# A hybrid encoder layer on one core: the input norm moves behind the projections as a factor per token

## The chip, the cores and the metric

The kernel runs on one core of a Trainium2 chip. The metric is the time of one execution in microseconds (us) on the device. Engines are named as the profile names them: PE (the matrix engine, with its weight loads PEld), DVE (VectorE), ACT (ScalarE), POOL (GpSimd) and SP, whose queue issues most transfers. Each engine works through its own instructions in a fixed order and waits where an operand is not there yet.

## The reference

2304 tokens of width 1024 (2048 of one request, 256 of another) go through one layer and a final norm, all in float32:

```
h = rmsnorm(x, norm1_w);  p = h @ w_in          # mq mk mv mo (512 each), gates 32, aq 512, ak 128, av 128
m_out = mlstm_mixer(mq, mk, mv, mo, gates, ...) # 8 heads, both directions
    # i, f from gates + b_gates;  v from mv;  out = sigmoid(mo) * norm(h_f + h_b) * mh_norm_w
a_out = attention_mixer(aq, ak, av, ...)
    # q = rope(rmsnorm(aq, q_norm_w)), k = rope(rmsnorm(ak, k_norm_w)) per head of 64;  8 query heads, 2 of keys
x = x + concat(m_out, a_out) @ w_out
h = rmsnorm(x, norm2_w);  x = x + (silu(g) * a) @ w_down,  [a, g] = conv3(h @ w_up)
y = rmsnorm(x, final_norm_w)
rmsnorm(x, w) = x * rsqrt(mean(x * x) + 1e-6) * w
```

## The kernel before

Every large matmul is done as three products of rounded parts (high x high, high x low, low x high), so each operand is kept as a pair. The token tiles are 128 wide: 18 of them, `order` = 16, 17 (the short request), then 0 to 15.

The first stage is `phase_a`. For each tile `front(i)` loads x with channels on the partitions (from `xT`, 512 bytes in a row), squares it on ACT (L183), adds the eight channel chunks on POOL (L189, L190; for the first tile on DVE, L186), sums over the partitions with a matmul by ones (L128), takes the power -1/2 on POOL (L142), spreads the result over the partitions with a second matmul (L144), multiplies x by it on DVE (L192), and splits that into the pair `n1T` (L193 on ACT, L194 on DVE). The pair is stored to `n_d` for the mLSTM part (L195) and used at once by `mm` (L236): 48 matmuls per tile, 24 of 512 columns and 24 of 288, into one PSUM tile `pj`, of which there are two. `weights` loads and splits the eight chunks `w_a` (L104, L105, L109); the same lines split the mLSTM weights `wm` later.

`post1` works on `pj`: it copies q and k to SBUF (L244), splits v (L247, L248), adds the gate bias (L251), squares q and k (L254), sums per head (L256), takes the power on POOL (L97, L98), multiplies (L258), and rotates: the cosine products on DVE (L264), four sine products on POOL (L270), their sum on DVE (L272). Then q and k are split (L274, L275, L278, L279) and stored. `post2` transposes k (L309). `gates` works on the gates of four tiles at a time, transposes them (L302) and copies the result into `rows` (L303). `tables` and `tables2` build the rotation tables `tab` (L214 to L223). `gate_math` follows the last tile: two scans over `rows` (L354, L356), transposes (L390), and the tables for the mLSTM.

After that two streams share the engines. `mlstm` handles four pairs of heads; `proj` reads `n_d` back and makes `mj` (L698, keys and queries) and `mv` (L708, values and the output gate `og`, L712), `proj_kv` and `proj_qo` do the same for the last pair. `attention` works in blocks of 512 queries: scores `ps` (L563, L564), row maxima `px` (L540, L542), exponentials (L567 to L569), values `pv` (L580 to L582), result to `mix_d`. When the mLSTM is finished, `phase_c` multiplies by `w_out`: 8 loads `cmx` of `mix_d` (L940, L941) and 192 matmuls `po` (L963) for each of nine blocks of 256 tokens, then adds x (L970), and norms (`rs_c`, L128, L144, L975 to L982). The first matmuls of the up-projection (`pa`, `pb`, `pc`, L1120) come between them and after them.

What stands where on an engine is set by a scheduler, which simulates the program with costs of its own and writes down one list per engine; `run_both` deals out the steps of the two streams by fixed numbers. A change of any instruction's cost in the simulation can therefore move others far behind it.

## Time and profile before

| | us |
|---|---|
| median of three runs (lowest, highest) | 3363.43 (3363.26, 3368.52) |
| the profiled execution, its own time | 3364.37 |
| its span | 3362.7 |
| PE busy | 3256.9 (97%) |
| DVE busy | 2473.1 (74%) |
| ACT busy | 1993.4 (59%) |
| POOL busy | 603.9 (18%) |

The times in the prediction's rows count from the start of the span. A row of the timeline gives start, length, engine, line, operation, tile written and read, number of instructions, and in brackets the idle time ahead of it with what ended it. A row of a line gives the shortest, median and longest duration in ns. A row of a stretch gives its length, then per engine the busy time and the number of instructions, the clock granted to PE, the busy share of the DMA engines and the rate in GB/s.

### The profile page before, as it was taken

The numbers are of one execution on the slowest core, as the hardware profiler recorded it, in microseconds if no ns is written. First come the engines' busy times: TensorE is split into PE (matmuls) and PEld (weight loads), VectorE is DVE, ScalarE is ACT, GpSimd is POOL, SyncE is SP. The second block draws the span as 40 slices with busy tenths as digits, with TensorE's granted clock in tenths as the row PEclk, the third lists the DMA queues.
The fourth block names the chain that finished last, engine by engine and source line by source line (L and its number), as shares of the span: only waits on it lengthen the run. The fifth ranks groups of instructions, "written<-read, shape, count | busy, mean of one in ns | idle before, by whom it ended". The sixth has DMA issues, their size and how long they took to land.

```text
span 3362.7 us, 53401 instructions
## 1 busy us (share of the span) xinstructions
PE 3256.9 (97%) x19566; PEld 3034.9 (90%) x19566; DVE 2473.1 (74%) x3736; ACT 1993.4 (59%) x3708; POOL 603.9 (18%) x1001
## 2 busy tenths in 40 slices
PE   7989999999999999999998899999999999999998
PEld 6778888888888888789887899999999999999998
DVE  7874576677657768876565899998888888666664
ACT  4535666666666776664444556665667667554543
POOL 7774032213215322200000000000000000020101
PEclk9999999999999999999998999999999999999999
DMA  8756343343337343332225656667666657968673
GB/s 247 215 182 186 106 124 93 107 126 102 103 102 237 111 131 121 122 115 95 86 96 184 239 208 223 219 239 275 227 238 236 212 192 258 317 225 277 225 241 114
DMA packets 393878, 601.68 MB, mean 179 GB/s; under 512 B 31248, under 2 KB 254640, under 8 KB 393616
## 3 DMA queue, kind: packets, MB, share of 16 engines
q1 hardware_dynamic: 360304, 552.51, 49.2%
q0 software_dynamic: 11856, 33.96, 3.7%
q10 hardware_dynamic: 21456, 11.80, 1.2%
q8 instruction: 154, 2.52, 0.3%
q14 instruction: 108, 0.88, 0.1%
HBM read 434.23 MB, written 163.92 MB: 178 GB/s over the span
## 4 chain that ended last, share of the span: by engine, by line
PE 77%; issue 6%; DMA 5%; POOL 4%; DVE 4%; ACT 3%; SPq 0%; POOLq 0%; DVEq 0%; ACTq 0%
PE pa L1120 16%; PE pc L1120 8%; PE po L963 6%; PE pf L1379 5%; PE pb L1120 4%; PE mj L698 4%; PE mv L708 4%; PE pv L580 3%; PE ps L563 3%; PE pv L582 3%; PE pv L581 3%; PE ps L564 3%; PE ph L1379 3%; PE px L540 3%; PE pg L1379 2%
## 5 line engine op out<-in xcount | busy, mean ns | idle before, releaser
L569 DVE TENSOR_TENSOR xx<-pe,xx 128x1024 fp32r<-128x1024 f32 x260 | 321.3, 1236 | 154.3 <-ACT xx L568 152.9
L567 ACT ACTIVATE pe<-ps 128x1024 f32<-128x1024 f32 x260 | 266.3, 1024 | 241.4 <-PE ps L564 237.8
L542 DVE TENSOR_REDUCE mx<-px 128x1 f32<-128x1024 f32 x256 | 310.6, 1218 | 88.2 <-PE px L540 86.4
L1337 POOL TENSOR_TENSOR sq<-sq,sq 128x384 f32<-128x384 f32 x38 | 49.5, 1303 | 1375.5 <-ACT sq L1333 1229.4
L568 ACT ACTIVATE xx<-pe 128x1024 fp32r<-128x1024 f32 x260 | 275.1, 1058 | 5.6
L963 PEld LDWEIGHTS po<-cmx,wo 128*128 128x128 f32 x1728 | 235.7, 193 | 38.3 <-ACT cmx L940 12.7
L963 PE MATMUL po<-cmx,wo 128*128 128x256 f32 x1728 | 244.0, 286 | 18.3 <-ACT cmx L940 12.1
L1124 ACT ACTIVATE u<-pa 128x386 f32<-128x386 f32 (+2 forms) x264 | 129.2, 490 | 173.7 <-PE pa L1120 170.2
L563 PE MATMUL ps<-qq,kk 128*128 128x512 f32 x520 | 213.0, 410 | 8.2 <-ACT pe L567 3.2
L580 PE MATMUL pv<-xx,vv 128*128 128x512 f32 x520 | 211.6, 407 | 3.4 <-ACT xx L568 2.0
L582 PE MATMUL pv<-xx,vv 128*128 128x512 f32 x520 | 211.7, 407 | 2.4 <-DVE xx L569 2.3
L581 PE MATMUL pv<-xx,vl 128*64 128x512 f32 x520 | 208.2, 400 | 0.0
L564 PE MATMUL ps<-qm,kl 65*128 65x512 f32 x520 | 206.5, 397 | 0.0
L698 PEld LDWEIGHTS mj<-mn,wm 128*128 128x128 f32 x1296 | 179.9, 193 | 20.1 <-ACT og L712 6.2
L698 PE MATMUL mj<-mn,wm 128*128 128x256 f32 x1296 | 192.1, 288 | 3.8 <-ACT og L712 3.7
L708 PE MATMUL mv<-wm,mn 128*128 128x256 f32 x1296 | 190.8, 285 | 0.7 <-ACT qb L704 0.7
L708 PEld LDWEIGHTS mv<-wm,mn 128*128 128x128 f32 x1296 | 176.5, 190 | 14.5 <-ACT qb L704 1.0
L236 PE MATMUL pj<-w_a,n1T 128*128 128x512 f32 (+1 forms) x864 | 178.8, 361 | 10.0 <-DVE n1T L194 6.7
L236 PEld LDWEIGHTS pj<-w_a,n1T 128*128 128x128 f32 x864 | 144.0, 196 | 30.2 <-DVE n1T L194 7.6
L540 PE MATMUL px<-kk,qq 128*128 128x512 f32 x512 | 166.6, 406 | 3.4 <-ACT pe L567 1.7
L802 ACT ACTIVATE dm<-dm,tm 128x128 f32<-128x128 f32 x288 | 95.8, 392 | 95.9 <-POOL dm L799 90.0
L1120 PE MATMUL pc<-nt,wb 128*128 128x386 f32 (+2 forms) x792 | 147.8, 341 | 0.0
(333 smaller groups left out, 8246.9 us busy)
## 6 DMA issues: line engine op xcount, KB each, us to landing
mn<-n_d SPq DMA_DIRECT2D x216, 256.0 KB, 3.2
ru<-w_up SPq DMA_DIRECT2D x88, 512.0 KB, 5.2
rs<-wsu_d SPq DMA_DIRECT2D x88, 512.0 KB, 5.6
act_d<-ts SPq DMA_DIRECT2D x33, 768.0 KB, 6.1
nt<-act_d SPq DMA_DIRECT2D x60, 384.0 KB, 5.0
re_t<-wsd_d SPq DMA_DIRECT2D x45, 512.0 KB, 5.0
wsu_d<-tw SPq DMA_DIRECT2D x44, 512.0 KB, 4.3
act_d<-ya SPq DMA_DIRECT2D x99, 192.0 KB, 2.8
```

The source lines that it names most:

```text
L236: nc.tensor.matmul(pjs[t][:, c0:c1], nTs[tiles[t]][:, c, a, :], ws[c][:, b, c0:c1], start=(c == 0 and k == 0), stop=(c == NCC - 1 and k == 2))
L542: nc.vector.tensor_reduce(s.mx[:, t0, z0:z0 + 1], ps, AX.X, ALU.max)
L563: nc.tensor.matmul(o, kk[:, kc:kc + P], s.qq, start=True, stop=False)
L569: nc.vector.tensor_tensor(x[:, 1], pe, f32(x[:, 0]), ALU.subtract)
L580: nc.tensor.matmul(s.pv, vv[:, kt % 4, :], x1, start=kt == 0, stop=False)
L581: nc.tensor.matmul(s.pv[0:HD], vl[:, kt % 4, :], x1, start=False, stop=False)
L582: nc.tensor.matmul(s.pv, vv[:, kt % 4, :], x2, start=False, stop=kt == s.nk - 1)
L698: nc.tensor.matmul(pj[:, o], s.w[c][:, a, o * P:(o + 1) * P], nT[c][:, h, :], start=(c + o + k == 0), stop=(c == NCC - 1 and k == 2 and o ...
L708: nc.tensor.matmul(pv[:, o], nT[c][:, a, o * P:(o + 1) * P], s.w[c][:, h, 256:512], start=(c + o + k == 0), stop=(c == NCC - 1 and k == 2 ...
L963: nc.tensor.matmul(po[:, o], wo[c][z // 2][:, a, n], mx[c][:, h, :], start=c + o + k == 0, stop=c == NCC - 1 and o == 1 and k == 2)
L1120: s.nc.tensor.matmul(p, w[:, aa, c, :], ops[k][:, c, bb, 0:s.n], start=c == 0 and i == 0 and not add, stop=c == NCC // 2 - 1 and i == 2, s ...
L1379: nc.tensor.matmul(ps[c], w[:, aa, c, :], t[:, gi - g0, bb, 0:H], start=gi == 0 and m == 0 and not more, stop=gi == NG - 1 and m == 2, ski ...
```

## The change

`front` no longer norms: it loads x from a copy with 4096 bytes in a row per partition (`xA`), and splits it. The 1/rms of a token, `g.rt`, comes from a second load of x with tokens on the partitions (`xR`), squared and summed by one ACT instruction; three small POOL instructions follow. Since `norm1_w` is already in the weights, every projection comes out too large by the token's rms, and the factor is applied afterwards: to v and the gates in `post1`, to the mLSTM's v and output gate in `proj`, `vback` and `proj_qo`, and as a logarithm (`g.lnr`) to the gates' exponents for the keys and to `nm` for the queries. The norm of q and k takes up the factor by a changed epsilon. The rotation reads `pj` in PSUM, its sine products are on DVE, and the norm's factor comes after the sum. `n_d` is stored in rows of 1024 bytes instead of 512. There are three PSUM tiles `pj`. The first two tiles' matmuls are issued together, weight chunk by weight chunk, and `mm` of a tile is issued one tile earlier than before.

```diff
         def front(i):
...
-            nc.sync.dma_start(x, g.xT[b, :, :, c0:c0 + P])
-            xq = sx.tile([P, NCC, P], F32, tag="xq", name=f"xq{i}", bufs=2)
-            nc.scalar.activation(xq, x, AF.Square, scale=1.0 / 32.0)
...
-                for k in (4, 2):
-                    nc.gpsimd.tensor_tensor(xq[:, 0:k], xq[:, 0:k], xq[:, k:2 * k], ALU.add)
-                nc.gpsimd.tensor_tensor(sq, xq[:, 0], xq[:, 1], ALU.add)
-            r = rstd_bc(g, sf, pp if n else pj_, [sq], P, "rs" if n else "pj", f"a{i}", bufs=2)
-            nc.vector.tensor_tensor(x, x, r.unsqueeze(1).to_broadcast([P, NCC, P]), ALU.mult)
+            nc.sync.dma_start(x, g.xA[i])
             nc.scalar.activation(nT[:, :, 0, :], x, AF.Copy)
             nc.vector.tensor_tensor(nT[:, :, 1, :], x, f32(nT[:, :, 0, :]), ALU.subtract)
-            g.st.dma_start(g.n1_d[b, :, :, :, c0:c0 + P], f32(nT))
+
+        def norm(i):
+            b, o = i // 2, i % 2
+            xr = sx.tile([P, D], F32, tag="xr", name=f"xr{i}", bufs=2)
+            nc.sync.dma_start(xr, g.xR[i])
+            g.st.dma_start(g.n1_d[b, :, :, o], f32(nTs[i]))
+            z = sp.tile([P, 2], F32, tag="ms1", name=f"ms1_{i}", bufs=4)
+            nc.scalar.activation(xr, xr, AF.Square, scale=1.0 / 32.0, accum_out=z[:, 0:1])
+            nc.gpsimd.tensor_scalar(z[:, 0:1], z[:, 0:1], EPS, None, ALU.add)
+            nc.gpsimd.tensor_scalar(z[:, 1:2], z[:, 0:1], EPS, None, ALU.mult)
+            nc.gpsimd.tensor_tensor(g.rt[:, i:i + 1], z[:, 0:1], g.mhalf[:, 0:1], ALU.pow)
+            ms1[i] = z
...
         def post1(i, pj):
-            nc.scalar.activation(qk, pj[:, 0:640].rearrange("p (h d) -> p h d", d=HD), AF.Copy)
+            u = pj[:, 0:640].rearrange("p (h d) -> p h d", d=HD)
+            nc.scalar.activation(xh, u, AF.Square, scale=0.125)
...
-            nc.vector.tensor_tensor(xh, qk, r.unsqueeze(2).to_broadcast([P, 10, HD]), ALU.mult)
...
-                nc.vector.tensor_tensor(t1[:, h0:h1, :], xh[:, h0:h1, :],
+                nc.vector.tensor_tensor(t1[:, h0:h1, :], u[:, h0:h1, :],
                                         tab[:, ti, a, 0:1, :].to_broadcast([P, n, HD]), ALU.mult)
...
-                    nc.gpsimd.tensor_tensor(half(t2[:, h0:h1, :], q), half(xh[:, h0:h1, :], 1 - q),
+                    nc.vector.tensor_tensor(half(t2[:, h0:h1, :], q), half(u[:, h0:h1, :], 1 - q),
                                             sin.to_broadcast([P, n, 2, 16]), ALU.mult)
             nc.vector.tensor_tensor(t1, t1, t2, ALU.add)
+            nc.vector.tensor_tensor(t1, t1, r.unsqueeze(2).to_broadcast([P, 10, HD]), ALU.mult)
...
         def gates(i0, n):
+            nc.scalar.activation(g.lnr[:, i0:i0 + n], g.rt[:, i0:i0 + n], AF.Ln)
...
-                nc.vector.tensor_copy(g.rows[:, :, i * P:(i + 1) * P], pg)
+                nc.scalar.activation(g.rows[:, :, i * P:(i + 1) * P], pg, AF.Copy)
...
     def proj(s, b):
...
-        nc.scalar.activation(og, pv[:, :, P:BT], AF.Tanh, scale=0.5)
+        for o in range(2):
+            nc.scalar.activation(og[:, o], pv[:, o, P:BT], AF.Tanh, scale=g.rh[:, 2 * b + o:2 * b + o + 1])
...
     def proj_qo(s, b):
...
-        nc.scalar.activation(og, pj[:, 1], AF.Tanh, scale=0.5)
+        rb = s1.tile([P, 2, P], F32, tag="og", name=f"rb{b}", bufs=1)
+        nc.sync.dma_start(rb, g.nm_d[2 * b:2 * b + 2, 16].unsqueeze(0).to_broadcast([P, 2, P]))
+        nc.vector.tensor_tensor(og, pj[:, 1], rb.rearrange("p n t -> p (n t)"), ALU.mult)
+        nc.scalar.activation(og, og, AF.Tanh, scale=0.5)
```

How the lists of the engines change shows at three places. (A number behind an underscore tells tiles of one name apart, and x3 is three instructions of one kind; the first tile's pair is `n1T_147` before and `n1T_151` after.) First, PE at the start of the program, before:

```order
L128 MATMUL rs_a_153<-ones,sq_151 128x2
L144 MATMUL rs_a_153<-ident,rcol_a_155 128x128
L236 MATMUL pj_248<-w_a_131,n1T_147 128x512 x2
L128 MATMUL rs_a_180<-ones,sq_176 128x2
L236 MATMUL pj_248<-w_a_131,n1T_147 128x512
L236 MATMUL pj_248<-w_a_131,n1T_147 128x288 x3
L236 MATMUL pj_248<-w_a_132,n1T_147 128x512 x3
L236 MATMUL pj_248<-w_a_132,n1T_147 128x288 x3
```

and after, where `pj_237` is the second tile's:

```order
L237 MATMUL pj_236<-w_a_135,n1T_151 128x512 x3
L237 MATMUL pj_236<-w_a_135,n1T_151 128x288 x3
L237 MATMUL pj_236<-w_a_136,n1T_151 128x512 x3
L237 MATMUL pj_236<-w_a_136,n1T_151 128x288 x3
L237 MATMUL pj_237<-w_a_135,n1T_161 128x512 x2
L237 MATMUL pj_236<-w_a_137,n1T_151 128x512
L237 MATMUL pj_237<-w_a_135,n1T_161 128x512
L237 MATMUL pj_237<-w_a_135,n1T_161 128x288 x3
```

The norm's matmuls are gone, and the second tile follows the first chunk by chunk.

Second, DVE ahead of the split of the fourth tile. Before, this is `n1T_297`, behind two norm multiplications (L192) and work of the first two tiles (`t_16`, `xh_436`, `gp`):

```order
L192 TENSOR_TENSOR x_298<-x_298,rs_a_306 128x1024
L295 SCALAR_TENSOR_TENSOR gtm<-gtm,t_16_460 128x2x16
L192 TENSOR_TENSOR x_401<-x_401,rs_a_409 128x1024
L258 TENSOR_TENSOR xh_436<-qk_429,rqk_440 128x640
L109 SCALAR_TENSOR_TENSOR wm_7_2448<-rm_7_0_2477,nw,wm_7_2448 128x512
L298 COPY gp_129<-gtm 128x4x8
L298 COPY gp_130<-gtm 128x4x8
L194 TENSOR_TENSOR n1T_297<-x_298,n1T_297 128x8x128
```

and after, `n1T_334`:

```order
L266 TENSOR_TENSOR t_17_464<-pj_237,tab 128x512
L272 TENSOR_TENSOR t_16_364<-pj_236,tab 128x16x16 x2
L266 TENSOR_TENSOR t_16_363<-pj_236,tab 128x128
L272 TENSOR_TENSOR t_16_364<-pj_236,tab 128x4x16 x2
L109 SCALAR_TENSOR_TENSOR wm_0_2312<-rm_0_0_2320,nw,wm_0_2312 128x512
L109 SCALAR_TENSOR_TENSOR wm_1_2313<-rm_1_0_2324,nw,wm_1_2313 128x512
L290 SCALAR_TENSOR_TENSOR t_16_481<-gtm 128x32
L184 TENSOR_TENSOR n1T_334<-x_335,n1T_334 128x8x128
```

The split no longer has the norm's multiplications ahead of it, but rotation products of both first tiles and two weight splits.

Third, PE where the attention ends (its last three instructions are L580 to L582 before, L593 to L595 after), before:

```order
L580 MATMUL pv_12_19778<-xx_12_7_19972,vv_16_12_10656 128x512
L581 MATMUL pv_12_19778<-xx_12_7_19972,vl_16_12_10657 64x512
L582 MATMUL pv_12_19778<-xx_12_7_19972,vv_16_12_10656 128x512
L144 MATMUL rs_c_20580<-ident,rcol_c_20583 128x128 x2
L963 MATMUL po_0_20481<-cmx_7_20441,wo_0_17320 128x256
L963 MATMUL po_1_20482<-cmx_7_20441,wo_0_17320 128x256
```

and after:

```order
L593 MATMUL pv_12_19712<-xx_12_7_19906,vv_16_12_10550 128x512
L594 MATMUL pv_12_19712<-xx_12_7_19906,vl_16_12_10551 64x512
L595 MATMUL pv_12_19712<-xx_12_7_19906,vv_16_12_10550 128x512
L983 MATMUL po_3_19951<-cmx_3_19223,wo_1_17163 128x256 x2
L983 MATMUL po_3_19951<-cmx_4_19227,wo_1_17189 128x256 x3
L983 MATMUL po_3_19951<-cmx_5_19231,wo_1_17199 128x256 x3
L983 MATMUL po_3_19951<-cmx_6_19235,wo_1_17245 128x256 x3
```

Before, the next matmuls use `cmx_7_20441`, which is loaded from what the last attention block wrote. After, the rest of one block of `po` (38 matmuls), a whole block (192) and 84 matmuls of a third stand between the attention's end and the tile that needs its result; 614 matmuls `po` are left at that point, against 300 before. The last block's norm, `rs_c`, had 44 matmuls `pa` and `pb` between it and the last `po`, and now none: they stand ahead of the last block.

More of the change, by code (lines that the diff above doesn't have):

```diff
@@ L226, in mm @@
         def mm(*tiles):
-            pjs = [pj_.tile([P, 1024], F32, tag="pj", name=f"pj{i}", bufs=2) for i in tiles]
+            pjs = [pj_.tile([P, 1024], F32, tag="pj", name=f"pj{i}", bufs=3) for i in tiles]
             cols = ((0, 512), (512, 800))
@@ L313, in phase_a @@
         front(order[0])
-        weights(range(0, 3))
+        weights(range(0, 2))
         front(order[1])
-        weights(range(3, 6))
+        weights(range(2, NCC))
         front(order[2])
-        weights(range(6, NCC))
+        for i in order[0:2]:
+            norm(i)
         tables()
         tables2(slice(0, 2))
+        norm(order[2])
+        pjs = mm(*order[0:2])
         prev = None
         for n, i in enumerate(order):
-            pj, = mm(i)
+            if 0 < n < NT - 1:
+                pjs += mm(order[n + 1])
             if n + 3 < NT:
                 front(order[n + 3])
+                norm(order[n + 3])
                 if n + 4 == NT:
@@ L692, in proj @@
         nm = f"{s.p}_{b}"
-        nT = [sn.tile([P, 2, BT], F32R, tag="nT", name=f"mn{nm}_{c}", bufs=NTB) for c in range(NCC)]
+        nT = [sn.tile([P, 2, 2, P], F32R, tag="nT", name=f"mn{nm}_{c}", bufs=NTB) for c in range(NCC)]
         for c in range(NCC):
@@ L718, in proj_halves @@
         nm = f"{s.p}_{b}"
-        nT = [sn.tile([P, 2, BT], F32R, tag="nT", name=f"{name}n{nm}_{c}", bufs=NTB) for c in range(NCC)]
+        nT = [sn.tile([P, 2, 2, P], F32R, tag="nT", name=f"{name}n{nm}_{c}", bufs=NTB) for c in range(NCC)]
         for c in range(NCC):
```

68 lines of the change are left out of this document (39 added, 29 removed).

## The prediction

> **What bounds the kernel now.** I read the stretches of 100 us first, then PE's timeline where PE isn't full.
>
> ```profile
> 0.00:100.00 100.00, 76.12 (x380) 64.08 (x381) 81.22 (x129) 50.03 (x72) 76.61 (x96) 0.95 0.78 234
> 100.00:200.00 100.00, 90.61 (x511) 78.03 (x510) 84.63 (x147) 49.52 (x83) 80.02 (x91) 0.98 0.72 212
> 200.00:300.00 100.00, 91.17 (x644) 83.34 (x643) 56.44 (x98) 38.85 (x90) 72.39 (x136) 0.97 0.71 215
> ...
> 1400.00:1500.00 100.00, 92.58 (x524) 75.40 (x523) 78.00 (x130) 63.85 (x104) 7.28 (x13) 0.98 0.28 90
> ...
> 1800.00:1900.00 100.00, 73.22 (x475) 71.69 (x474) 66.48 (x115) 33.88 (x52) 4.38 (x6) 0.85 0.77 270
> ```
>
> The columns are PE, PEld, DVE, ACT and POOL busy, then the clock granted to PE, the DMA share and GB/s. PE is busy for 3256.9 of 3362.7 us; of the 105.8 us of idle time, 42 lie in the first 300 us and 27 in the stretch from 1800. So the change pays where it fills these holes, and elsewhere only what PE itself does counts.
>
> ```profile
> 14.46 1.22 PE L236 MATMUL pj<-w_a,n1T 128*128 128x512 f32 x2 [2.40 <-ACT n1T L193]
> ...
> 24.54 4.01 PE L236 MATMUL pj<-w_a,n1T 128*128 128x512 f32 x20
> 33.16 7.90 PE L236 MATMUL pj<-w_a,n1T 128*128 128x512 f32 x22 [4.61 <-DVE n1T L194]
> ...
> 59.58 7.15 PE L236 MATMUL pj<-w_a,n1T 128*128 128x512 f32 x25 [1.14 <-DVE n1T L194]
> ...
> 157.26 6.67 PE L236 MATMUL pj<-w_a,n1T 128*128 128x512 f32 x30
> 163.77 0.38 PE L144 MATMUL rs_a<-ident,rcol_a 128*128 128x128 f32 x2
> ...
> 164.11 6.73 PE L236 MATMUL pj<-w_a,n1T 128*128 128x288 f32 x36
> ...
> 220.62 3.51 PE L698 MATMUL mj<-mn,wm 128*128 128x256 f32 x28
> ```
>
> The projections run from 14.5 to 220.6 us. In undisturbed stretches they are fast: 66 matmuls (42 of 512 columns, 24 of 288) take 6.65 + 6.57 us, 0.222 and 0.162 us each, so a tile's 24 + 24 need 9.2 us and 18 tiles 166. The fourth tile starts in earnest at 59.6, and the last fifteen take (220.6 - 59.6) / 15 = 10.73 us each. The mLSTM's `mj` follows without a gap, so the end of this stage is what counts for all that follows.
>
> **The start.** `front` now waits for no sum, power or multiplication.
>
> ```profile
> 5.78 1.06 ACT L183 ACTIVATE xq<-first 128x1024 f32<-128x1024 f32 x1 [3.70 <-DMA first<-xT]
> 22.10 1.74 DVE L214 COPY rot<-qkw 128x16 f32<-128x16 f32 x8 [0.78 <-DMA qkw<-q_norm_w]
> L194 DVE TENSOR_TENSOR n1T<-x,n1T x16: 1204/1218/1776, 43.9 to 202.7; 128x1024 fp32r<-128x1024 f32 x16
> L109 DVE SCALAR_TENSOR_TENSOR w_a<-first,nw,w_a 128x800 fp32r<-128x800 f32 x6 | 6.5, 1092 | 0.0
> L109 DVE SCALAR_TENSOR_TENSOR wm<-rm,nw,wm 128x512 fp32r<-128x512 f32 x8 | 7.7, 980 | 1.4 <-ACT wm L105 1.4
> L223 DVE TENSOR_TENSOR tab<-tab,qkw 128x128 f32<-128x128 f32 x6 | 3.0, 500 | 0.0
> 35.00:40.00 5.00, 5.00 (x16) 3.93 (x15) 2.92 (x2) 1.15 (x2) 4.83 (x5) 0.63 0.90 261
> ```
>
> x lands at 5.8; a split on ACT (1.06, the same size), one on DVE (1.2) and a weight split (1.09) give the first matmul near 9.5 instead of 14.5. DVE needs 2 x 1.2 + 8 x 1.09 = 11.1 us for both pairs and all weights, less than the 18.4 us of the 96 matmuls, so these are PE's own: the first two tiles end near 28.5 (before: 24.54 + 4.01 for one), the third at 37.7. Then comes a hole. The rotation tables now queue behind two loads of x (0.52 MB each) and one `n_d` (1.05 MB), which at 299 GB/s (below) is 7 us, so `rot` starts near 28.5 instead of 22.1. DVE then does `rot` and two scalings (2.3), twelve table products (6.0), the first tiles' parts that stand ahead of `n1T_334` (two reductions, five or six products, two `wm` splits; by the rows here and below 8.6 with the split itself): it is ready at about 45. PE idles for 7 us, and then pays for a lowered clock: in the stretch 35 to 40, after an idle 4.6 us, 0.63 was granted, and 22 matmuls took 7.90 us instead of 4.9, a price of 3.0. The page TensorE: Matmul & The Clock Gate of the Trainium skill (What's actually happening) has half clock after about 3.4 us of idling until about 3.4 us of work are done. The trace agrees in kind; by the page the price would be an estimated 1.7 us, and the two such holes of this sum would cost 2.6 us less. At 59.58 the kernel before paid 7.15 - 25 x 0.222 = 1.6 of the same kind. Lead at the fourth tile: 59.6 - 45 - (3.0 - 1.6) = 13 us.
>
> **The steady tiles.** On PE, 36 + 36 norm matmuls go: the two of L144 hold up the next by 0.14 us (163.77 to 163.91), and L128 the same. What stays beside the 9.2 us is `pk` and `pg`, like them 0.14 each: 9.5 us; with the 0.95 to 0.98 granted above, 9.75. Can DVE keep up? Shortest, median and longest ns, then means by shape:
>
> ```profile
> L264 DVE TENSOR_TENSOR t<-xh,tab x34: 275/819/1666, 45.0 to 221.7; 128x512 f32<-128x512 f32 x17, 128x128 f32<-128x128 f32 x17
> L272 DVE TENSOR_TENSOR t<-t,t x17: 804/826/1908, 48.7 to 223.7; 128x640 f32<-128x640 f32 x17
> L256 DVE TENSOR_REDUCE ms<-xh x18: 801/806/821, 33.3 to 226.3; 128x10 f32<-128x640 f32 x18
> L275 DVE TENSOR_TENSOR qz<-t,qz x17: 672/680/777, 50.3 to 225.3; 128x512 fp32r<-128x512 f32 x17
> L279 DVE TENSOR_TENSOR kz<-t,kz x17: 274/284/1373, 50.9 to 226.0; 128x128 fp32r<-128x128 f32 x17
> L248 DVE TENSOR_TENSOR v<-pj,v x18: 229/278/294, 33.0 to 224.8; 128x128 fp32r<-128x128 f32 x18
> L264 DVE TENSOR_TENSOR t<-xh,tab 128x128 f32<-128x128 f32 x17 | 11.7, 687 | 0.0
> L270 POOL TENSOR_TENSOR t<-xh,tab 128x256 f32<-128x256 f32 x34 | 34.4, 1033 | 10.3 <-DVE xh L258 10.3
> L98 POOL TENSOR_TENSOR rqk<-rqk,mhalf 128x10 f32<-128x10 f32 x18 | 37.9, 2108 | 0.7
> ```
>
> L264 of 128 columns takes 0.275 at best and 0.687 in the mean, because POOL's L270 runs beside it; L270 goes. The new sine products are unseen on DVE. From below they cost nothing (no reason has them free), from above what they cost POOL (1.03 for 256 columns); nearest are DVE's own rows, 0.28 for 128 and 0.68 for 512, so 0.41 for 256 and 0.21 for 64, 1.24 in all. A tile then costs DVE 1.22 (split) + 0.81 + 0.28 + 0.18 + 0.68 + 0.28 + 1.24 + 2 x 0.83 + 0.68 + 0.28 = 7.3, the gates some 0.8 (eleven instructions for four tiles at 0.28), `wm` 0.98 x 8 / 18 = 0.44: 8.5, under 9.75. The new epilogue multiplication only replaces L258; L192 (a read of as many columns as L194) and L303 are gone. Against the change speaks VectorE: DVE Perf Modes of the Trainium skill (Rules for kernel authors): copy from PSUM first if many operations read it; its errata table has 62 cycles more for a PSUM source, an estimated 0.065 us. Here L248 reads PSUM, with 0.278 no slower than L279's 0.284 from SBUF. By the page six more PSUM reads make 8.9 a tile, still under 9.75, so the sum stays and the rival below gains a little. POOL keeps the power (2.1) and 1.5 of small work and loses the rest. ACT trades the square of x for that of `xr`, loses L244, gains `rows` and half a table load a tile: 6 us. The third `pj` covers the wait for the power: between a tile's end and the reuse of its bank lie two tiles, 19 us, and DVE is about 11 behind.
>
> The added loads go through SP's queue:
>
> ```profile
> DMA packets 89633, 51.16 MB, mean 218 GB/s; under 512 B 2576, under 2 KB 86288, under 8 KB 89616
> ...
> q1 hardware_dynamic: 80096, 46.37, 66.0%
> ```
>
> That is to 235 us. SP's queue moved 46.37 MB in 66.0% of the time, 299 GB/s when busy. With 9.4 MB more, 60.6 MB would need 203 us at that rate: room for 32 us of gain, not more. A packet of 579 bytes cost 0.66 x 235 x 16 / 80096 = 31 ns; x in 4096-byte rows and `n_d` in 1024-byte rows make fewer, at between one (free length) and two times (all length) the old cost for `n_d`. I take the transfers as just hidden. Fifteen tiles gain 15 x (10.73 - 9.75) = 14.7 us.
>
> **Behind the stage** `gate_math` is the same chain, but PE's list has the transposes of the scan ahead of the second `mj`.
>
> ```profile
> 237.40 4.51 DVE L354 TENSOR_TENSOR_SCAN rows<-rows 8x2048 f32<-8x2048 f32 x1
> ...
> 241.94 5.47 PE L698 MATMUL mj<-mn,wm 128*128 128x256 f32 x31 [2.22 <-ACT og L712]
> ```
>
> Two scans of 4.5 follow the last gates, so the transposes wait some 2 us beyond the 2.22 already lost: -2 us. The split tanh (27 times 128 columns more) and `proj_qo`'s product (9 times about 0.41) lie beside attention matmuls: nothing, and if that cover is gone, 27 x 0.2 + 9 x 0.4 = 9 us. A late product would keep PE from the next `mj`, since that has one bank.
>
> **The end of the attention** moves by the scheduler.
>
> ```profile
> 1801.71 0.61 PE L144 MATMUL rs_c<-ident,rcol_c 128*128 128x128 f32 x4
> 1812.72 15.09 PE L963 MATMUL po<-cmx,wo 128*128 128x256 f32 x108 [10.41 <-ACT cmx L940]
> 1832.13 8.35 PE L963 MATMUL po<-cmx,wo 128*128 128x256 f32 x48 [4.32 <-DVE cx L970]
> ...
> 1848.71 11.65 PE L963 MATMUL po<-cmx,wo 128*128 128x256 f32 x96 [0.92 <-DVE cx L970]
> ...
> 1876.14 1.01 PE L128 MATMUL rs_c<-ones,cacc 128*128 128x2 f32 x4 [7.97 <-DVE cacc L978]
> 1880.32 1.23 PE L144 MATMUL rs_c<-ident,rcol_c 128*128 128x128 f32 x4 [3.16 <-DVE rcol_c L140]
> 1881.20 6.33 PE L1120 MATMUL pc<-nt,wb 128*128 128x386 f32 x24
> ```
>
> Idle before: 10.41 + 4.32 + 0.92 + 7.97 + 3.16 = 26.8, and slow clock: at 11.65 / 96 = 0.121 a matmul the rows of 108 and 48 lost 2.0 and 2.5, that of `pc` about 1.9: 33 in all. After, 314 matmuls (38 us) stand between the attention and `cmx_7`: 10.41 is covered, and the 48 `pa`, `pb` cover the 4.32. In exchange nothing covers the last norm: 1848.71 + 11.65 to 1880.32 is 20.0 us, now all idle, with 3 for the clock and 2 of small waits: 25. Gain 8 us, bounds 0 and 14.
>
> **Sum.** 13 + 14.7 - 2 + 8 = 33.7 from the profiled execution's 3364.4 (its span, 3362.7, and 1.7 around it; the median of the runs is 3363.4, 0.9 less): 3331 us.
>
> **Rivals.** *DVE or the DMA binds the steady tiles* (0.24). For: three resources at 8.5 to 9.75 of a period. If DVE stays at its contended means, or the DMA can't fill above nine tenths, a tile needs 10.5 and more, and 13 + 2 - 2 + 5 = 18 are left: 3346. *The ideal* (0.05): no hole at the fourth tile, 9.5 a tile, 14 at the attention's end: about 3310. *Slower* (0.07): the second load turns into a wait. v and the gates need `rt`, thus `xr`, which SP issues behind a store of `n_d`; ACT waits for it with splits of later tiles behind it. A tile moves 3.0 MB; the lead of 13 - 2 + 8 = 19 is used up at 10.73 + 19 / 15 = 12.0 us a tile, that is below 250 GB/s, and the mean of the stage before was 218. Against it: that rate had idle queues, x is issued three tiles ahead. At 215 GB/s it would be 14 a tile, 3395. *No change* (0.04): the work behind the stage waits for something else than PE; the rows from 300 on, 98% PE, speak against it: 3364.
>
> **Numbers.** The first case has 0.60, from 3318 (attention's end 14, tiles at 9.5) to 3344 (none there, tiles at 9.95). A difference under 0.2% (6.7 us) I count as none, about what a measurement of this kernel can tell. Faster: 0.60 + 0.24 + 0.05. The range 3311 to 3352 leaves out the slower and the unchanged cases and the ends of the others.
>
> **What would show it.** Right: first projection near 9.5, `mj` starting at 190 to 195, DVE's 128-column product near 0.28, no long idle after the last `pv`, one of some 20 us ahead of `rs_c`. Wrong: matmuls waiting for banks of `pj` (DVE late) or for `n1T` behind loads, a DMA share above 0.9 in the first 200 us, or attention matmuls that wait for exponentials where fewer `po` lie between them, as in the stretch from 1400.

## The result, and the profile after

| | before | after |
|---|---|---|
| median of four runs, us (lowest, highest) | 3365.51 (3363.26, 3368.52) | 3343.48 (3337.43, 3350.44) |
| profiled execution, us (span) | 3364.37 (3362.7) | 3337.43 (3335.7) |
| PE busy, us | 3256.9 | 3248.2 |

The ratio of the times is 0.9935, with an interval of 0.9913 to 0.9956: 15 to 29 us faster, 22 by the medians, 27 by the two profiled executions. The forecast was 3331, with a range of 3311 to 3352.

The stretches of 100 us of the changed kernel, columns as in the prediction:

```profile
0.00:100.00 100.00, 90.28 (x472) 77.71 (x473) 76.98 (x172) 59.23 (x97) 46.72 (x72) 0.98 1.02 355
100.00:200.00 100.00, 93.22 (x566) 82.24 (x564) 78.17 (x182) 54.56 (x116) 53.48 (x87) 1.00 0.87 275
200.00:300.00 100.00, 93.06 (x651) 84.49 (x652) 44.08 (x66) 49.20 (x121) 37.06 (x86) 0.97 0.55 158
...
1000.00:1100.00 100.00, 91.45 (x547) 79.28 (x546) 75.36 (x151) 58.66 (x142) 29.04 (x61) 0.93 0.53 166
...
1800.00:1900.00 100.00, 81.91 (x519) 81.30 (x518) 72.90 (x112) 44.81 (x69) 3.65 (x5) 0.90 0.63 224
```

POOL falls from 76.6 to 46.7 in the first stretch, and the transfers rise from 234 to 355 GB/s. A new hole stands at 1000 to 1100, where the kernel before had PE busy for 98.0 us at full clock:

```profile
1000.00:1100.00 100.00, 97.99 (x647) 85.98 (x645) 77.96 (x167) 69.17 (x167) 47.18 (x98) 1.00 0.74 220
```

PE's timeline of the changed kernel:

```profile
6.99 0.80 PE L237 MATMUL pj<-w_a,n1T 128*128 128x512 f32 x1 [6.99 <-ACT w_a L105]
8.21 28.55 PE L237 MATMUL pj<-w_a,n1T 128*128 128x512 f32 x143 [0.43 <-DVE w_a L109]
37.23 0.71 PE L237 MATMUL pj<-w_a,n1T 128*128 128x512 f32 x2 [0.46 <-DVE t L272]
39.78 13.63 PE L237 MATMUL pj<-w_a,n1T 128*128 128x512 f32 x61 [1.84 <-DVE n1T L184]
...
177.27 1.02 PE L237 MATMUL pj<-w_a,n1T 128*128 128x288 f32 x6
178.43 0.36 PE L313 MATMUL pk<-identr,kz 128*128 128x128 f32 x2
178.63 3.22 PE L711 MATMUL mj<-mn,wm 128*128 128x256 f32 x25
...
201.05 0.86 PE L401 MATMUL gpt<-ident,rows 40*128 40x40 f32 x6 [3.34 <-DVE rows L365]
...
1009.71 1.22 PE L553 MATMUL px<-kk,qq 128*128 128x512 f32 x2 [2.08 <-ACT pe L580]
...
1020.99 0.50 PE L739 MATMUL mj<-mjn,wm 128*128 128x256 f32 x2 [1.14 <-ACT wm L105]
...
1029.03 0.63 PE L566 MATMUL pr<-identr,m4r 128*128 128x128 f32 x4 [2.46 <-DVE m4r L563]
...
1744.20 0.39 PE L595 MATMUL pv<-xx,vv 128*128 128x512 f32 x1
...
1816.12 13.79 PE L983 MATMUL po<-cmx,wo 128*128 128x256 f32 x114
1837.59 1.01 PE L128 MATMUL rs_c<-ones,cacc 128*128 128x2 f32 x4 [7.68 <-DVE cacc L998]
1848.91 1.22 PE L144 MATMUL rs_c<-ident,rcol_c 128*128 128x128 f32 x4 [10.30 <-DVE rcol_c L140]
1849.78 6.10 PE L1140 MATMUL pc<-nt,wb 128*128 128x386 f32 x24
```

Three marks divide the program: the first `mj`, the first `pc`, the end.

| us | before | after | difference |
|---|---|---|---|
| start to the first `mj` | 220.62 | 178.63 | -42.0 |
| first `mj` to the first `pc` | 1660.6 | 1671.2 | +10.6 |
| first `pc` to the end | 1481.5 | 1485.9 | +4.4 |

So the projections gained half again as much as forecast (27.7), and 15 us were given back behind them. Of the 42.0 us, 24.7 are idle time of PE (34.6 before, 9.9 after). The other 17.3 are PE's own busy time, 186.0 before and 168.8 after: the 72 matmuls of the norm are gone, and the granted clock is 0.99 in the mean instead of 0.97. In the stage itself DVE's split of x and the products and sums of the rotation cost what they were estimated at (lines by form, up to 195 us; busy time, then mean ns):

```profile
L184 DVE TENSOR_TENSOR n1T<-x,n1T 128x1024 fp32r<-128x1024 f32 x16 | 19.5, 1219 | 5.8 <-ACT n1T L183 5.7
...
L274 DVE TENSOR_TENSOR t<-t,t 128x640 f32<-128x640 f32 x18 | 14.7, 817 | 0.1
...
L272 DVE TENSOR_TENSOR t<-pj,tab 128x256 f32<-128x256 f32 x36 | 13.5, 413 | 0.0
...
L272 DVE TENSOR_TENSOR t<-pj,tab 128x64 f32<-128x64 f32 x36 | 6.2, 212 | 0.0
...
L266 DVE TENSOR_TENSOR t<-pj,tab 128x128 f32<-128x128 f32 x18 | 5.0, 279 | 0.0
```

The transfers of the same 195 us:

```profile
DMA packets 58867, 61.47 MB, mean 315 GB/s; under 512 B 2913, under 2 KB 50785, under 8 KB 58851
...
q1 hardware_dynamic: 49259, 56.52, 85.5%
```

### The profile page after: what moved, and what is told of

Read it like the earlier page. It is cut to its first block, busy times and chain, and to the rows that moved or that the text cites. A ratio compares the mean times of both kernels' runs of the same rounds, so it can differ in the third digit from the quotient of the medians.

```text
span 3335.7 us, 53337 instructions
## 1 busy us (share of the span) xinstructions
PE 3248.2 (97%) x19494; PEld 3025.2 (91%) x19494; DVE 2429.6 (73%) x3765; ACT 2003.1 (60%) x3769; POOL 512.4 (15%) x915
## 4 chain that ended last, share of the span: by engine, by line
PE 77%; issue 6%; DMA 5%; DVE 5%; ACT 4%; POOL 2%; SPq 0%; POOLq 0%; ACTq 0%; DVEq 0%
PE pa L1140 17%; PE pc L1140 8%; PE pf L1399 5%; PE po L983 5%; PE pj L237 5%; PE pb L1140 4%; PE mj L711 4%; PE mv L721 3%; PE ps L576 3%; PE ps L577 3%; PE pv L593 3%; PE pv L595 3%; PE pv L594 3%; PE px L553 2%; PE ph L1399 2%
## 5 line engine op out<-in xcount | busy, mean ns | idle before, releaser
L582 DVE TENSOR_TENSOR xx<-pe,xx 128x1024 fp32r<-128x1024 f32 x260 | 319.1, 1228 | 127.3 <-ACT xx L581 125.8
L580 ACT ACTIVATE pe<-ps 128x1024 f32<-128x1024 f32 x260 | 266.3, 1024 | 172.5 <-PE ps L577 163.4
L983 PEld LDWEIGHTS po<-cmx,wo 128*128 128x128 f32 x1728 | 227.3, 189 | 16.7 <-ACT wo L105 0.8
L1144 ACT ACTIVATE u<-pa 128x386 f32<-128x386 f32 (+2 forms) x264 | 129.0, 489 | 177.6 <-PE pa L1140 171.5
L983 PE MATMUL po<-cmx,wo 128*128 128x256 f32 x1728 | 234.3, 282 | 0.5 <-ACT wo L105 0.2
L593 PE MATMUL pv<-xx,vv 128*128 128x512 f32 x520 | 212.1, 408 | 6.6 <-ACT xx L581 3.9
L595 PE MATMUL pv<-xx,vv 128*128 128x512 f32 x520 | 211.0, 406 | 7.1 <-DVE xx L582 7.0
L711 PEld LDWEIGHTS mj<-mn,wm 128*128 128x128 f32 x1296 | 177.8, 192 | 16.9 <-ACT og L727 3.2
L711 PE MATMUL mj<-mn,wm 128*128 128x256 f32 x1296 | 190.6, 287 | 2.1 <-ACT og L727 2.1
L237 PE MATMUL pj<-w_a,n1T 128*128 128x512 f32 (+1 forms) x864 | 167.8, 353 | 9.7 <-ACT w_a L105 7.0
```

The lines of the kernel that those rows point to most:

```text
L237: nc.tensor.matmul(pjs[t][:, c0:c1], nTs[tiles[t]][:, c, a, :], ws[c][:, b, c0:c1], start=(c == 0 and k == 0), stop=(c == NCC - 1 and k == 2))
L582: nc.vector.tensor_tensor(x[:, 1], pe, f32(x[:, 0]), ALU.subtract)
L593: nc.tensor.matmul(s.pv, vv[:, kt % 4, :], x1, start=kt == 0, stop=False)
L595: nc.tensor.matmul(s.pv, vv[:, kt % 4, :], x2, start=False, stop=kt == s.nk - 1)
L711: nc.tensor.matmul(pj[:, o].rearrange("p (n t) -> p n t", t=P), s.w[c][:, a, o * P:(o + 1) * P], nT[c][:, :, h, :], start=(c + o + k == 0) ...
L983: nc.tensor.matmul(po[:, o], wo[c][z // 2][:, a, n], mx[c][:, h, :], start=c + o + k == 0, stop=c == NCC - 1 and o == 1 and k == 2)
```

## The experiments

The table has the ratio to the kernel before on the same chip with its interval, and from each profile the span, the first `mj`, and the time from there to the first `pc`. The two profiles of the changed kernel itself (here and `again`) agree within 1.4 us at all marks. Each profile is one execution, though, and the runs of one kernel lie up to 16 us apart, so a difference of some us behind the first `mj` can be chance.

| | ratio (interval) | span | first `mj` | `mj` to `pc` |
|---|---|---|---|---|
| before | | 3362.7 | 220.6 | 1660.6 |
| the change | 0.9935 (0.9913 to 0.9956) | 3335.7 | 178.6 | 1671.2 |
| again | 0.9928 (0.9916 to 0.9941) | 3337.1 | 178.9 | 1671.9 |
| old_order | 0.9924 (0.9912 to 0.9936) | 3342.4 | 185.1 | 1670.0 |
| sine_on_pool | 0.9941 (0.9929 to 0.9953) | 3350.6 | 190.6 | 1674.6 |
| hold_up | 0.9933 (0.9920 to 0.9945) | 3344.3 | 179.9 | 1677.9 |
| one_load | 0.9918 (0.9901 to 0.9934) | 3339.7 | 181.7 | 1674.0 |
| two_more | 0.9995 (0.9986 to 1.0004) | 3363.2 | 223.0 | 1656.0 |
| short_rows | 0.9948 (0.9927 to 0.9968) | 3340.8 | 185.9 | 1672.7 |
| sine_alone | 0.9940 (0.9922 to 0.9958) | 3346.6 | 214.1 | 1648.5 |
| norm_off | 0.9972 (0.9962 to 0.9981) | 3352.2 | 215.7 | 1658.1 |
| no_factor | 0.9904 (0.9890 to 0.9917) | 3337.8 | 180.3 | 1671.3 |
| lead_14 | 0.9922 (0.9909 to 0.9936) | 3336.0 | 178.7 | 1675.8 |
| lead_15 | 0.9917 (0.9904 to 0.9930) | 3346.6 | 178.6 | 1681.0 |

### What brought the projections forward

**again**

> The changed kernel once more. Its first profile had the first mj of the mLSTM at 178.6 us and a span of 3335.7, while the four times lay between 3337 and 3350. If the gain of the projections is firm and the spread comes from later stages, mj starts within 1 us of 178.6 again, and a difference in the span lies behind 300 us. If the start itself varies (transfers run at 350 GB/s there), mj moves by several us.

`mj` starts at 178.9: the stage is firm. This profile is again near the lowest of its runs (3336.8 to 3351.6), so no profile shows where the longer runs spend their time.

**old_order**: `mm` tile by tile, two banks.

```diff
...
-        pjs = mm(*order[0:2])
...
-            if 0 < n < NT - 1:
-                pjs += mm(order[n + 1])
+            pj, = mm(i)
...
```

> The changed kernel with the old order of the projections: mm is issued tile by tile, one tile later, and with two banks of pj. My theory, that the missing norm and POOL's missing products brought the gain: a single first tile is paced by the weight splits on DVE (1.05 us each) as closely as by its own six matmuls (1.15 us), so little is lost at the start, and the tiles stay near 9.3 us: mj at 179 to 184. The rival, that the early order and the third bank carry it: DVE is about 10 us behind PE, so with two banks a tile waits for the products that read its bank: 10 us and more a tile, mj at 190 or later. The end of the attention here has the order of the kernel before (300 po behind the last pv, 48 pa and pb behind the last po), so the total can differ by some us for that reason alone.

`mj` starts at 185.1, just behind the range. But the steady tiles don't suffer: from 60 to 160 us PE is busy without a gap, with two banks and the old order. The time is lost in one hole ahead of the third tile:

```profile
35.50 0.34 DVE L272 TENSOR_TENSOR t<-pj,tab 128x64 f32<-128x64 f32 x2
...
35.99 12.91 PE L237 MATMUL pj<-w_a,n1T 128*128 128x512 f32 x53 [8.58 <-DVE t L290]
```

With two banks the third tile has to use the first tile's. DVE's first row is the end of the rotation products that read this bank; they had waited for the tables, and PE starts 0.15 us behind them. (L290, which the profile names, is the next instruction on DVE and reads no `pj`.) So this is the rival's mechanism, at the start alone: in the changed kernel the third bank lets the third tile go ahead of the tables. What the early issue is worth by itself wasn't measured, and of the total nothing can be told.

**sine_on_pool**

```diff
...
+            nc.scalar.activation(qk, u, AF.Copy)
...
-                    nc.vector.tensor_tensor(half(t2[:, h0:h1, :], q), half(u[:, h0:h1, :], 1 - q),
+                    nc.gpsimd.tensor_tensor(half(t2[:, h0:h1, :], q), half(qk[:, h0:h1, :], 1 - q),
```

> The changed kernel with the four sine products back on POOL (from a copy of q and k in SBUF, made by ACT as before). If POOL's products slow DVE down: the 128-column cosine product goes from 0.28 us to some 0.69 in the mean, the sum from 0.82 to about 1.18. My theory, that DVE is not what bounds the tiles (8.5 of 9.24 us, and the contention eats what the sine products free): mj at 178 to 183. The rival, that the contention bound the tiles before: above 10 us a tile, mj at 192 or later.

`mj` comes at 190.6, 12.0 later, between the two ranges. The expected slowing of the cosine product didn't come. DVE's pair of cosine products (512 and 128 columns) beside work of POOL, first in the kernel before:

```profile
100.74 3.23 POOL L189 TENSOR_TENSOR xq<-xq 128x512 f32<-128x512 f32 x2 [0.59 <-ACT xq L183]
...
102.68 1.43 DVE L264 TENSOR_TENSOR t<-xh,tab 128x512 f32<-128x512 f32 x2
```

and in this one:

```profile
103.29 2.57 POOL L274 TENSOR_TENSOR t<-qk,tab 128x256 f32<-128x256 f32 x4 [7.63 <-DVE t L276]
...
103.48 0.88 DVE L268 TENSOR_TENSOR t<-pj,tab 128x512 f32<-128x512 f32 x2
104.28 1.12 DVE L277 TENSOR_TENSOR t<-t,rqk 128x640 f32<-128x640 f32 x1
```

With both inputs in SBUF the pair took 1.43 us beside POOL's sums. With one in PSUM it takes 0.88 in the middle of POOL's products, as its parts do undisturbed (0.68 and 0.28, which overlap a little). The two POOL operations differ, so the next row is the closer comparison: the multiplication right behind the pair reads SBUF alone, beside the same POOL products, and takes 1.12 us instead of 0.83. What costs the 12 us was not isolated. POOL's row shows a likely part: it waited 7.63 us for DVE's sum of the tile before, which holds the one buffer of `t2`, so its products came late.

**sine_alone**: the kernel before, with this one line of the change.

```diff
-                    nc.gpsimd.tensor_tensor(half(t2[:, h0:h1, :], q), half(xh[:, h0:h1, :], 1 - q),
+                    nc.vector.tensor_tensor(half(t2[:, h0:h1, :], q), half(xh[:, h0:h1, :], 1 - q),
```

> The kernel before with one part of the change: the four sine products on DVE (from the normed q and k in SBUF), everything else as it was. Putting them back on POOL in the changed kernel cost 12.0 us of the stage. My theory, that this part is worth as much by itself: mj at 206 to 213 instead of 220.6. The rival, that without the other parts DVE, which keeps the norm's multiplication of 1.2 us a tile, is the bound, or that the norm's chain on POOL still holds the tiles: mj at 216 to 224. Its end of the attention has 427 po behind the last pv, so the total can differ for that reason.

**norm_off**: the kernel before without one line.

```diff
-            nc.vector.tensor_tensor(x, x, r.unsqueeze(1).to_broadcast([P, NCC, P]), ALU.mult)
```

> The kernel before with one instruction a tile left out, the multiplication of x by its factor (L192), so x is projected without its norm and the outputs lack it; the sum, the power and both norm matmuls are still made, for nothing. So nothing of the projections waits for the norm any more, but POOL and PE still do its work, and the sine products are still on POOL. The changed kernel's mj came 42 us earlier, of which the sine products' place accounts for 6.5 (alone) to 12 (last). My theory, that most of the rest is the norm's wait: the first projection near 8 to 10 us instead of 14.5, and mj at 195 to 208. The rival, that the tiles were bound by POOL's and DVE's queues in any case, since matmuls L144 in PE's list still wait for the power: only the start is gained, 4 to 8 us, mj at 212 to 217. Its end of the attention has the order of sine_alone (427 po behind the last pv).

The products alone bring `mj` to 214.1 (6.5 earlier, 1 us outside the range expected), the norm alone to 215.7 (5.0 earlier: the rival's range). Together with the rest of the change it is 42. (In the whole, this tells little: the one line of `sine_alone` measures 0.9940, which can't be told from the 0.9935 of the whole change, because its stretch from `mj` to `pc` is 12 us shorter than before. Why it is shorter wasn't found.) The stretch from 60 to 160 us shows what stays busy in each, with the columns as ever (PE, PEld, DVE, ACT, POOL, clock, DMA share, GB/s); in the kernel before:

```profile
60.00:160.00 100.00, 91.84 (x512) 78.80 (x512) 87.64 (x145) 48.67 (x80) 82.85 (x91) 0.99 0.75 220
```

with the products alone on DVE:

```profile
60.00:160.00 100.00, 92.92 (x524) 80.13 (x523) 87.95 (x187) 49.05 (x81) 62.82 (x55) 0.99 0.78 226
```

with the norm's multiplication alone taken out:

```profile
60.00:160.00 100.00, 86.31 (x484) 72.81 (x485) 74.52 (x132) 47.66 (x79) 87.42 (x98) 1.00 0.72 210
```

and in the changed kernel:

```profile
60.00:160.00 100.00, 100.00 (x571) 87.94 (x570) 77.61 (x184) 58.61 (x117) 47.97 (x55) 1.00 1.01 337
```

Before, DVE at 88% and POOL at 83% handed work to each other tile by tile, and PE waited for either. Moving the products leaves DVE at 88%; taking out the multiplication leaves POOL at 87%, with the norm's matmuls still in PE's list waiting for it. In the changed kernel both queues are relieved, and PE runs without a gap. That it takes these two together is the likely reading, but it isn't shown by itself: no run makes just these two changes, and the changed kernel has no norm matmuls in PE's list either.

### The transfers

**one_load**

```diff
...
-            nc.sync.dma_start(xr, g.xR[i])
...
-            nc.scalar.activation(xr, xr, AF.Square, scale=1.0 / 32.0, accum_out=z[:, 0:1])
+            nc.scalar.activation(xr, xs.pop(i).rearrange("p c t -> p (c t)"), AF.Square, scale=1.0 / 32.0, accum_out=z[:, 0:1])
```

> The changed kernel without the second load of x: the square and its sum are taken over the first load, which leaves out the right factor per token (the sum then runs over the tokens of a chunk), and saves 18 transfers of 0.52 MB. The DMA share is 1.03 to 1.08 from 40 to 140 us in the changed kernel, so the second load could hold the projections up. My theory, that PE bounds the tiles there (it idles 2.3 us behind 30 us): only the tables come some 3 us earlier and close the two small holes at 37 and 39 us, mj at 175 to 178.6. The rival, that the saturated transfers cost time: mj at 172 or earlier.

**two_more**

```diff
             nc.sync.dma_start(xr, g.xR[i])
+            xz = sx.tile([P, D], F32, tag="xz", name=f"xz{i}", bufs=1)
+            nc.sync.dma_start(xz, g.xR[i])
```

> The changed kernel with a third load of x: each second load is made twice, into another tile that nothing reads; 9.4 MB more. At the 355 GB/s that the first 100 us show this is 26.6 us of transfers. My theory, that the stage still has room for transfers only behind 140 us (shares of 0.88 and 0.76 there, some 10 us): n1T comes late, and mj starts at 188 to 196. The rival, that the share above 1 is early work for the mLSTM which simply moves back: mj at 179 to 182. This kernel's end of the attention has another order (309 po behind the last pv), so its total says less than its mj.

**short_rows**

```diff
-            nc.sync.dma_start(x, g.xA[i])
+            nc.sync.dma_start(x, g.xT[b, :, :, o * P:o * P + P])
```

> The changed kernel with x for the projections loaded in rows of 512 bytes as before, instead of 4096. At the 31 ns that a packet took before, 1024 packets over 16 engines need 2.0 us against 1.5 us for 0.52 MB at 355 GB/s: 18 x 0.5 = 9 us more of transfers. My theory, that the row length is a help and not what carries the gain: mj at 179 to 185. The rival, that the transfers bound the tiles before and the long rows brought the gain: mj at 190 or later.

Without the second load nothing is gained: the projections end at 177.6 (178.3 with it), `mj` at 181.7 is 3 us later by a wait of 3.73 us for a key's split, and the holes at the start stay. So the load is hidden, and neither range was right. With a third load the transfers are no longer hidden:

```profile
45.42 11.28 PE L239 MATMUL pj<-w_a,n1T 128*128 128x512 f32 x49 [8.88 <-DVE t L274]
...
126.33 8.20 PE L239 MATMUL pj<-w_a,n1T 128*128 128x512 f32 x24 [5.83 <-DVE t L274]
...
188.71 4.37 PE L239 MATMUL pj<-w_a,n1T 128*128 128x512 f32 x28
...
215.53 0.86 PE L403 MATMUL gpt<-ident,rows 40*128 40x40 f32 x6 [8.89 <-DVE rows L367]
```

The projections end at 188.71 + 4.37 = 193.1 instead of 178.3, with two holes. Ahead of the first, the tables come late: DVE waited 5.90 us for ACT, and ACT 5.67 us for a load of x. Ahead of the second, DVE waited 6.29 us for ACT's half of a later tile's split, and the products that free the bank stood behind it. Since this list has `gpt` ahead of `mj`, the scan adds its wait: `mj` at 223.0, beyond both ranges, and the whole gain is gone. In `short_rows` (`mj` at 185.9, 1 us outside the range of my theory) PE is busy for 99.9 of 100 us from 60 to 160. Of the 7.2 us, 4.5 are lost at the start, where the tables' first copy runs at 29.6 instead of 26.2 and the fourth tile waits 6.0 us; the other 2.7 are a wait for a key's split behind the last tile. So the long rows help at the start, and rows of 512 bytes don't hold the steady tiles up.

### What was given back

**hold_up**

```diff
...
+            nc.scalar.activation(first[0].p1[:, 0:2], g.xl[2][:, 0, 0:2], AF.Copy)
             first[0].mul(first[0].p1, "11", ops)
```

> The changed kernel with one small ACT copy that keeps the first 48 matmuls of the up-projection (pa, pb) back until the last block's third po is added; PE's list is the same up to there, and the 48 stand between the last po and rs_c. My theory, that the 7.7 and 10.3 us of idle time ahead of rs_c are only for want of matmuls: 48 x 0.178 = 8.5 us of them are covered, and a little of the slow clock; 8 to 11 us faster than the changed kernel. The rival, that what follows rs_c (weights split on DVE and ACT) is the bound there: PE waits as long, only elsewhere, and the time is within 2 us.

The rival was right. The 48 matmuls cover the wait for `cacc`, and no gain is seen:

```profile
1793.68 5.22 PE L983 MATMUL po<-cmx,wo 128*128 128x256 f32 x30 [2.92 <-DVE cx L990]
...
1811.29 8.63 PE L983 MATMUL po<-cmx,wo 128*128 128x256 f32 x48 [4.08 <-DVE cx L990]
...
1844.13 2.28 PE L1141 MATMUL pb<-n,wa 128*128 128x386 f32 x12
1846.25 0.50 PE L128 MATMUL rs_c<-ones,cacc 128*128 128x2 f32 x4
1856.92 1.22 PE L144 MATMUL rs_c<-ident,rcol_c 128*128 128x128 f32 x4 [10.17 <-DVE rcol_c L140]
```

Taken from their old place, the matmuls leave 2.92 and 4.08 us open there, and `rs_c` waits for DVE as before. From the end of the last `po` to the second `rs_c` it takes 19.0 us, as long as in the changed kernel (19.0, without a matmul between them) and hardly less than in the kernel before (20.0, with 44). DVE's own timeline has no idle time from the last addition of x to the power of the norm:

```profile
1837.96 0.69 DVE L990 TENSOR_TENSOR cx<-po,cx 128x512 f32<-128x512 f32 x1 [3.56 <-PE po L983]
...
1854.16 1.84 DVE L1066 TENSOR_TENSOR nt<-nt 128x772 fp32r<-128x772 f32 x2
1855.90 0.17 DVE L136 RECIPROCAL rcol_c<-rcol_c 128x2 f32<-128x2 f32 x1
```

These 18 us are splits and sums for the up-projection that stand ahead of the norm in DVE's list, in the kernel before too.

**no_factor**

```diff
-        for o in range(2):
-            nc.scalar.activation(og[:, o], pv[:, o, P:BT], AF.Tanh, scale=g.rh[:, 2 * b + o:2 * b + o + 1])
+        nc.scalar.activation(og, pv[:, :, P:BT], AF.Tanh, scale=0.5)
...
-        nc.vector.tensor_tensor(og, pj[:, 1], rb.rearrange("p n t -> p (n t)"), ALU.mult)
...
```

> The changed kernel without the factor per token in the mLSTM stream (one tanh instead of two, one copy to va for the last pair, no transfer and product rb), so those outputs lack the factor. From the first mj to the first pc the changed kernel takes 1671 us, the kernel before 1661. My theory, that these 10 us come from the order in which the two streams meet on DVE (the hole from 1009 to 1033 us, where DVE is full of row maxima, weight splits and the state C) and not from the added instructions: this stretch differs from 1671 only as far as the order does (427 po behind the last pv here instead of 614), in either direction, by up to 12 us. The rival, that the added instructions cost it: the two waits at 1179 and 1252 us for va and ogT go, the hole from 1009 to 1033 too, and the stretch is at or below 1661 us.

**lead_14**, **lead_15**

```diff
-LEAD = 1.3
+LEAD = 1.4    # lead_15: 1.5
```

> The changed kernel with one number of the dealing changed: LEAD 1.4 instead of 1.3, by which the mLSTM's steps are dealt out further ahead of the attention's; no instruction is added or removed. 462 po are left behind the last pv instead of 614, and all 48 pa and pb stand behind the last po. My theory, that order alone moves the stretch from mj to pc by 10 us and more: mj stays at 178 to 180 and the stretch comes to 1645 to 1665 instead of 1671, so 3320 to 3340 us in all. The rival, that the stretch is set by the work of PE, DVE and the transfers in it: within 4 us of 1671.

> The same with LEAD 1.5: 300 po are left behind the last pv and 48 pa and pb behind the last po, as in the kernel before, with the wait for cmx that this had (10.4 and 4.3 us). My theory: the end costs about as much as before (33 us of waits and slow clock, against some 20 in the changed kernel), the middle changes by its order, 1650 to 1680 us from mj to pc; what it cannot do is change mj by more than 1 us. The rival, that the middle is unmoved and only the end counts: 8 us slower than the changed kernel.

Without the added instructions the stretch takes 1671.3: they are not what costs it, though the waits for `va` and `ogT` at 1179 and 1252 go with them (all but 0.28 us). The hole near 1020 is there too, only at other places (4.14 us at 1008, 3.21 at 1038). In the changed kernel it is DVE's:

```profile
1010.00:1020.00 10.00, 9.85 (x56) 8.63 (x55) 8.64 (x17) 5.31 (x14) 1.10 (x2) 0.85 0.82 270
1020.00:1030.00 10.00, 6.02 (x26) 4.21 (x26) 9.89 (x20) 1.70 (x3) 1.04 (x2) 0.83 0.50 165
1030.00:1040.00 10.00, 9.54 (x40) 8.26 (x40) 5.24 (x14) 6.18 (x16) 2.84 (x7) 0.66 0.19 54
```

DVE is busy for 9.89 of 10 us with row maxima, the last pair's weight splits and the state `C`, and ACT for 1.70; the clock granted from 1030 to 1040 is 0.66. But a hole there doesn't decide the stretch: `sine_alone` has PE busy for only 92.3 of the same 100 us, and the shortest stretch of all. My theory for the rest fell, too: with LEAD 1.4 the stretch takes 1675.8 and not 1645 to 1665, and with 1.5 it takes 1681.0 (with waits of 9.0 and 3.9 us for `cmx` and `cx` at its end, as foreseen). That the order moves it by 10 us isn't shown by these two either: the profiled run of `lead_15` is the slowest of its five (3348.3, median 3341.3), and by their ratios the two and the change (0.9922, 0.9917 and 0.9935) can't be told apart. All kernels that norm behind the projections and have `mj` ahead of `gpt` lie at 1670 to 1681, and the four others at 1648 to 1661. What these share stays open. The stretch holds the same matmuls before and after:

```profile
220.62:1881.20 1660.58, 1601.33 (x10209) 1408.42 (x10207) 1133.17 (x2003) 1007.47 (x2103) 376.26 (x755) 0.98 0.40 127
...
178.63:1849.78 1671.15, 1607.38 (x10208) 1408.66 (x10208) 1131.14 (x2010) 1021.98 (x2143) 366.74 (x742) 0.98 0.41 127
```

The first row is the kernel before, the second the changed one. Of the 10.6 us, 4.5 are idle time of PE and 6.1 are longer busy time, at the same mean clock. Not every kind of matmul is slower: in unbroken rows from 240 to 1250 us an `mj` takes 0.121 us against 0.124 before (medians of 33 and 40 rows of twelve and more, their length less 0.15 for the last one's end).

No kernel was shown to beat the change: the intervals of `lead_14`, `lead_15`, `old_order` and even `sine_alone` overlap with its own.

## Why the prediction came out as it did

- **The bound.** "The change pays where it fills these holes" held for the projections. Why the holes were there was told only in part: the sum priced waits one by one, while the parts measured alone gain 5.0 and 6.5 us and the whole 42. The likely reason is two queues, DVE and POOL, that had to be relieved together. In this stage the rival called ideal, at 0.05, was the nearest: no hole at the fourth tile and 9.5 us a tile make the same 42 us (59.6 - 37.7 + 1.6 + 15 x 1.23).
- **The start** (lead 13, measured 59.58 - 39.78 = 19.8). The first matmul came at 7.0, not 9.5, and the third tile ends at 36.8 (forecast 37.7). The step that was mis-sized is the hole ahead of the fourth tile, 0.46 + 1.84 us instead of 7. DVE's rows have it:

```profile
26.17 1.27 DVE L215 COPY rot<-qkw 128x16 f32<-128x16 f32 x8 [7.71 <-DMA qkw<-q_norm_w]
...
38.51 1.21 DVE L184 TENSOR_TENSOR n1T<-x,n1T 128x1024 fp32r<-128x1024 f32 x1
```

  Of the two waits, 0.46 us is for the bank of the first tile and 1.84 for the split. The split was ready at 39.7 and not at 45: `rot` ran at 26.2 instead of 28.5, and the work from there to the split's end took 13.5 us instead of 16.9. The price of the clock was about 1.5 us (13.63 for 61 matmuls, against 37 x 0.222 + 24 x 0.162 = 12.1 if 24 of them are short). From 40 to 44 us the granted clock was 0.57. The price is nearer to the 1.7 estimated from the Trainium skill, TensorE: Matmul & The Clock Gate (What's actually happening), than to the row that I took (3.0). The idling of about 3.4 us that this page names isn't seen here: gaps of 0.46 and 1.84 us were enough.
- **The steady tiles** (9.75, measured (178.3 - 39.8) / 15 = 9.23). The forecast took over a granted clock of 0.95 to 0.98; without idle gaps it is 1.00, and `pk` and `pg` fit into 9.5. Gain 22 instead of 14.7. DVE's new products cost 0.413 and 0.212 us (estimated 0.41 and 0.21), the 128-column product 0.279 (0.28). For many operations on a PSUM source, the Trainium skill's VectorE: DVE Perf Modes (Rules for kernel authors) has a copy first as one of two choices. The measurement shows no need of it here: the 128-column product takes 0.279 from PSUM, and 0.296 from SBUF in `sine_alone`.
- **The transfers.** "Just hidden" was right, by `one_load` and `two_more`. One sign of being wrong came without its harm: the DMA share was 1.02 in the first 100 us, above the 0.9 that a rival took for the limit, and PE ran without a gap from 60 to 160 all the same. The rate was not 299 but 339 GB/s (56.52 MB in 85.5% of 195 us), so the bound of 32 us on the gain, which I drew from it, was wrong. The rival of the second load as a wait needs one load more than the kernel has.
- **Behind the stage** (-2): the transposes of the scan wait 3.34 us, about as foreseen. But in the 80 us behind the first `mj` PE idles for 13.6 us instead of 7.5, so the term was about -6. Beside the 3.34, PE now waits there for a key's split (1.02), for the last gates (1.69 and 1.05) and for a load of v (1.70), to which I gave no price.
- **The end of the attention** (+8, of 33 us): the idle time went from 26.8 to 0.22 + 7.68 + 10.30 = 18.2, that is 8.6. Right in size, and wrong in one reason: I took the 20 us ahead of the second `rs_c` for a norm that lacks cover. They are DVE's queue, 19 to 20 us long with 44, 48 or no matmuls beside it. What was gained are the waits for `cmx` and `cx`.
- **Missing from the sum:** the stretch between. From 300 to 1700 us the waits of PE grew from 24.3 to 31.2 us, most of it from 1000 to 1100, PE was busy for 6 us longer with the same matmuls from `mj` to `pc`, and behind `pc` 4.4 us were lost. The last sentence of the prediction names "attention matmuls that wait for exponentials" as a sign, but gives it no price.
- **The range.** By the terms that the prediction gives for them, the ends of its first case come out as 3321 and 3342, not 3318 and 3344. The result, 3343, lies just beyond that upper end and inside the stated range.

That the total came within 13 us of the forecast is in part luck, since two errors of opposite sign met: 14 us too little for the projections, and some 20 too much behind them (+6 forecast, -15 measured).

## What to carry to other kernels

Where two engines hand each tile's work to one another and both are busy for over four fifths of the time, as here, a change that relieves one can show little, and its worth can't be read from what it removes: look at which queue stays full, and count the change as a whole. Before filling an idle stretch of PE, follow the engine that ends it: if that one has no idle time, more matmuls gain nothing. In a program ordered by a scheduler, the stage that was changed and the total are two questions, and the marks of the profile answer them separately. A profile is one execution, so compare it with the spread of the runs before a difference of some us is given a cause.

## What was not expected of the hardware

DVE's cosine products with one input in PSUM were not slowed by POOL's sine products (0.88 us for the pair), while a multiplication with both inputs in SBUF beside the same products was (1.12 instead of 0.83). In the kernel before, the 128-column product with both inputs in SBUF took 0.69 in the mean; with one in PSUM it took 0.28 in `sine_on_pool`. The Trainium skill, SBUF — State Buffer (Who interferes with whom), states this: a DVE instruction with two SBUF inputs contends with a GpSimd instruction that reads SBUF. The trace agrees for POOL's products, but such an instruction is not slowed each time: in the pair of 1.43 us beside POOL's sums, only the second product was slow (0.83; the first took 0.68). So here reading PSUM directly saved a slowdown beside the copy. And the transfers reached 355 GB/s over the first 100 us, with packets of 1232 bytes in the mean (35.47 MB in 28797), where the kernel before moved 299 when busy. The length of x's rows isn't what makes the rate: from 60 to 160 us `short_rows` moved 340 GB/s and the changed kernel 337.
